# Up projection of a hybrid decoder layer: a fourth home for split weights, and the convolution's taps one step sooner

## The chip, the cores and the metric

The kernel runs as one program on one core of a Trainium2 chip. The metric is the device time of one execution in microseconds (us). The core's engines work side by side, each through a queue of its own: TensorE (PE, matrix products, with its weight loads, PEld), VectorE (DVE), ScalarE (ACT), GpSimd (POOL), and SyncE (SP), which here issues nearly all transfers (DMA) from the chip's memory. Engines wait for each other by semaphores.

## The reference

One layer, batch 1, 256 tokens, width 2048, everything in float32. The part that matters here is the second half, a gated MLP with a causal convolution over three tokens:

```python
h = rmsnorm(x, norm_ffn_w[l])
gate, up = jnp.split(jnp.einsum('bsd,df->bsf', h, w_up[l]), 2, axis=-1)
gate = causal_dwconv(gate, conv_ffn_w[l]) + conv_ffn_b[l]
x = x + jnp.einsum('bsf,fd->bsd', jax.nn.gelu(gate, approximate=False) * up, w_down[l])
```

`w_up` is 2048 x 11264: 5632 columns of gate and 5632 of up. Ahead of it come the two token mixers (a gated delta rule and a causal pooling mixer) with their projections, behind it the down projection and a last norm. The change touches none of these.

## The kernel before

**Split weights.** Float32 products are made on PE from two parts. A weight tile `raw` (128 x 1024, 512 KB) is cast on ACT to a high part `whi` (L289), and DVE makes the low part `wlo` = raw − whi, the *split* (L297). PE then multiplies by the high part first and by the low part behind it (L1374). `raw` has four buffers, `whi` and `wlo` three each. A transfer into a `raw` buffer waits for the split of the tile that lay there, four tiles earlier. A cast into a `whi` buffer waits until PE has used the tile three earlier. `weights()` hands PE the next step's parts, and before that begins (loads, casts, splits) the steps up to AHEAD = 2 further on:

```python
def weights(ahead=AHEAD):
    begin(taken[0] + ahead + 1)
    taken[0] += 1
    return made[taken[0] - 1]
```

**Chunks and steps.** The up projection runs over 11 chunks c of 512 gate and 512 up columns. PE's order is written out by hand (`up_steps`); on ACT, DVE and the queues the order comes from a scheduler, which places each instruction when its operands and its buffer are expected to be ready, and from `issue_after`, which binds one instruction behind another. In chunks 1 to 7 and 9 one half of the contraction (two blocks of 512 rows, written /1 and /0) isn't multiplied plainly: seven products of sums of quarters take the place of eight. So one *group* of PE steps, which I name after the chunk whose plain steps open it, is: g1 to g4 (the four plain gate steps of chunk c, 12 matmuls each), u1 (the first plain up step), then the parts of chunk c+1, six matmuls each, between the other up steps: T1/1, u2, 11/1, u3, T1/0, 11/0, u4, T2/1, T2/0, 21/1, 21/0, the transposes of c's gate, T3/1, T3/0, 22/1, 22/0, the transposes of c's up, T4/1, T4/0. Plain steps load a `raw` tile; parts read quarters (`quad`) that were loaded ahead to homes of their own, or sums of quarters that DVE makes (L230, bound behind the last split). The same 22 steps come again for each group.

**What else is on DVE and ACT.** Behind the products "11" a bank is copied on ACT; ahead of "21" (L1396) and behind T3 (L1410) DVE adds a bank to the product T1, and the parts behind it go on adding to that new bank. When the last T4 of a group is out, a generator `elementwise` is set up. The plain steps that follow call it, one stage at a time: `gate_part` gives four blocks of columns, each with a convolution start on ACT (L1326) and two taps on DVE (L1331), and after these the gelu on ACT (L1335); `up_part` then multiplies by up (L1344) and splits the result into `hhi` (ACT, L1351) and `hlo` (DVE, L1352). Before the change the generator stops after the second block and after the gelu:

```python
            if f == 1:
                yield
```

Each result chunk c from 4 on has a home of its own, tags `hhi4` to `hhi10`, empty until chunk c is made. Tag `s` is another place of the same size.

Of the kernel before, what the change touches and what calls it, by code (L numbers as in the profile page):

```python
# [15 lines left out]
S = 256  # L16
# [19 lines left out]
def kernel(  # L36
# [91 lines left out]
    for step in up_steps:  # L128
        if step[0] == "plain":
            srcs.append(up_w[step[1]][step[2]][step[3]])  # L130
        elif step[0] == "part":
            srcs.append(("up", *step[1:]))
    sums_behind = {}
    for n, src in enumerate(srcs):
# [138 lines left out]
    def begin_half(n, k):  # L273
        high_half(n, k)
        low_half(n, k)

    def begin(n):
        while len(made) < min(len(srcs), n):
            load(len(made) + 1)
            raw = loads[len(made)]  # L280
            if isinstance(raw, tuple):
# [4 lines left out]
            keep = kept.get(len(made))  # L286
            hi = wpool.tile(shape, F32R, tag="whi", name=nm("whi")) if keep is None else \
                mtile(keep, shape, F32R, nm("khi"))
            nc.scalar.copy(hi, raw)  # L289
            if shape[1] == 8:  # L290
                lo = None
                nc.vector.tensor_tensor(hi[:, :, 32:64], raw[:, :, 0:32], hi[:, :, 0:32].bitcast(F32),
                                        op=ALU.subtract)
            else:
                lo = wpool.tile(shape, F32R, tag="wlo", name=nm("wlo")) if keep is None else \
                    mtile(4 + keep, shape, F32R, nm("klo"))
                last_split[0] = nc.vector.tensor_tensor(lo, raw, hi.bitcast(F32), op=ALU.subtract).ins  # L297
# [1021 lines left out]
    def gate_part(c, pts):  # L1319

        y = fp.tile([P, 4, S], F32, tag="y", name=nm("y"))
        for f in range(4):
            r = 4 * c + f
            pt = pts[f // 2][:, f % 2, :]
            with tc.issue_after(last_copy[0]) if c < NUP - 1 else ExitStack():
                nc.scalar.activation(y[:, f, :], pt, AF.Identity, scale=cfw[:, 2 * KF + r : 2 * KF + r + 1],  # L1326
                                     bias=vec[:, V_CB + r : V_CB + r + 1])
            with tc.issue_after(last_sum[0]) if c < NUP - 1 else ExitStack():
                for j in (1, 0):
                    s = 2 - j  # L1330
                    nc.vector.scalar_tensor_tensor(y[:, f, s:], pt[:, : S - s], cfw[:, j * KF + r : j * KF + r + 1],  # L1331
                                                   y[:, f, s:], op0=ALU.mult, op1=ALU.add)
            if f == 1:
                yield
# [42 lines left out]
    def up_product(c, what, ch):  # L1377
# [69 lines left out]
    for i, step in enumerate(up_steps):  # L1447
        if step[0] == "part":
            up_product(*step[1:])
            if step[2] == "T4" and step[3] == chunks_of[step[1]][-1]:  # L1450
# [227 lines left out]
```

## Time and profile before

| | |
|---|---|
| three runs | 1540.68, 1541.54, 1542.59 us |
| median | 1541.54 us |
| profiled execution | 1542.63 us, of which the span is 1540.8 |
| PE busy | 1526.0 us, 99% of the span |
| DVE busy | 1253.4 us, 81% |
| ACT busy | 849.8 us, 55% |
| up projection, with the first steps behind it | 820 to 1310 us of the span |

A row of a timeline gives the start in us, the length, engine, line, operation, what it writes and reads, and shapes; "x2" means that neighbouring instructions were drawn together; a bracket at the end is the idle time before it and what ended that. A matmul's row ends when its result is drained, so that neighbouring matmuls overlap. A row of waits gives an engine's line, what it waited for, the total, the number and the longest. Buffer numbers are left out of the names in profile rows.

### The profile page before, as it was taken

The numbers are of one execution on the slowest core, as the hardware profiler recorded it, in microseconds if no ns is written. First come the engines' busy times: TensorE is split into PE (matmuls) and PEld (weight loads), VectorE is DVE, ScalarE is ACT, GpSimd is POOL, SyncE is SP. The second block draws the span as 40 slices with busy tenths as digits, with TensorE's granted clock in tenths as the row PEclk, the third lists the DMA queues.
The fourth block names the chain that finished last, engine by engine and source line by source line (L and its number), as shares of the span: only waits on it lengthen the run. The fifth ranks groups of instructions, "written<-read, shape, count | busy, mean of one in ns | idle before, by whom it ended". The sixth has DMA issues, their size and how long they took to land.

```text
span 1540.8 us, 20209 instructions
## 1 busy us (share of the span) xinstructions
PE 1526.0 (99%) x7302; PEld 1257.4 (82%) x7302; DVE 1253.4 (81%) x1776; ACT 849.8 (55%) x1063; POOL 70.8 (5%) x90
## 2 busy tenths in 40 slices
PE   9999999999999999999999999999999999999998
PEld 8887888788878888788888888888788888888886
DVE  6788859896589858987667899999999886878885
ACT  7455446454455445454455676666667665555552
POOL 1010002000100000000000000000000000000100
PEclk9999999999999999999999999999999999999999
DMA  8776757776577766776578646666457467556652
GB/s 276 215 221 199 202 163 214 213 214 183 152 245 205 205 169 201 222 200 186 179 250 300 194 163 217 219 205 205 150 155 242 125 216 267 183 193 205 227 189 90
DMA packets 166674, 310.46 MB, mean 201 GB/s; under 512 B 19458, under 2 KB 23330, under 8 KB 166446
## 3 DMA queue, kind: packets, MB, share of 16 engines
q1 hardware_dynamic: 159456, 287.37, 60.0%
q0 software_dynamic: 5184, 18.88, 3.7%
q10 hardware_dynamic: 1934, 2.93, 0.5%
q8 instruction: 57, 0.93, 0.2%
q14 instruction: 43, 0.35, 0.1%
HBM read 301.75 MB, written 7.38 MB: 201 GB/s over the span
## 4 chain that ended last, share of the span: by engine, by line
PE 92%; DVE 4%; issue 2%; DMA 1%; ACT 0%; POOL 0%; POOLq 0%; DVEq 0%; ACTq 0%
PE psg L1374 25%; PE psm L334 15%; PE psm L332 14%; PE psm L333 14%; PE psm L1359 7%; PE psg L1359 7%; DVE wlo L297 3%; PE psm L1374 2%; PE psm L478 1%; PE psg L377 1%; DVE quad L230 1%; PE psm L1436 1%; DMA vrow<-ev 1%; PE psg L868 1%; DMA mv<-vrow 1%
## 5 line engine op out<-in xcount | busy, mean ns | idle before, releaser
L289 ACT CAST whi<-raw 128x1024 fp32r<-128x1024 f32 x428 | 450.0, 1052 | 428.4 <-PE psm L333 280.2
L297 DVE TENSOR_TENSOR wlo<-raw,whi 128x1024 fp32r<-128x1024 f32 x426 | 517.3, 1220 | 151.2 <-ACT whi L289 146.2
L289 ACT CAST whi<-quad 128x1024 fp32r<-128x1024 f32 x168 | 176.1, 1054 | 141.0 <-DVE quad L230 39.4
L297 DVE TENSOR_TENSOR wlo<-quad,whi 128x1024 fp32r<-128x1024 f32 x168 | 202.6, 1219 | 36.2 <-ACT whi L289 35.3
L334 PE MATMUL psm<-wlo,xhl 128*128 128x512 f32 x432 | 169.5, 393 | 1.6 <-DVE wlo L297 1.6
L332 PE MATMUL psm<-whi,xhl 128*128 128x512 f32 x432 | 169.0, 391 | 0.0
L333 PE MATMUL psm<-whi,xhl 128*128 128x512 f32 x432 | 168.6, 390 | 0.0
L1374 PE MATMUL psg<-whi,fhl 128*128 128x512 f32 x504 | 127.1, 389 | 0.0
L1374 PEld LDWEIGHTS psg<-whi,fhl 128*128 128x128 f32 x504 | 94.4, 188 | 19.5
L334 PEld LDWEIGHTS psm<-wlo,xhl 128*128 128x128 f32 x432 | 81.1, 188 | 19.0 <-DVE wlo L297 2.4
L333 PEld LDWEIGHTS psm<-whi,xhl 128*128 128x128 f32 x432 | 81.1, 188 | 16.8
L332 PEld LDWEIGHTS psm<-whi,xhl 128*128 128x128 f32 x432 | 81.1, 188 | 16.6
L230 DVE TENSOR_TENSOR quad<-quad,quad 128x1024 f32<-128x1024 f32 x72 | 87.6, 1217 | 0.0
L1374 PE MATMUL psg<-wlo,fhl 128*128 128x512 f32 x252 | 69.9, 389 | 0.0
L1374 PE MATMUL psg<-whi,ups 128*128 128x512 f32 x216 | 58.9, 394 | 0.0
L1359 PE MATMUL psm<-whi,hhi 128*128 128x512 f32 (+1 forms) x150 | 58.1, 387 | 0.0
L1359 PE MATMUL psm<-whi,hlo 128*128 128x512 f32 (+1 forms) x150 | 57.9, 386 | 0.0
L1359 PE MATMUL psm<-wlo,hhi 128*128 128x512 f32 (+1 forms) x150 | 57.4, 387 | 0.1
L1374 PEld LDWEIGHTS psg<-wlo,fhl 128*128 128x128 f32 x252 | 47.3, 188 | 9.8
L332 PE MATMUL psm<-whi,mhi 128*128 128x512 f32 x128 | 50.8, 397 | 0.0
L1359 PE MATMUL psg<-whi,hhi 128*128 128x512 f32 (+1 forms) x130 | 50.3, 387 | 0.4 <-ACT whi L289 0.4
L1359 PE MATMUL psg<-whi,hlo 128*128 128x512 f32 (+1 forms) x130 | 50.0, 386 | 0.0
(432 smaller groups left out, 2927.3 us busy)
## 6 DMA issues: line engine op xcount, KB each, us to landing
raw<-in_w_in_dram SPq DMA_DIRECT2D x224, 512.0 KB, 4.2
raw<-in_w_up_dram SPq DMA_DIRECT2D x104, 512.0 KB, 4.8
quad<-in_w_up_dram SPq DMA_DIRECT2D x72, 512.0 KB, 4.9
raw<-in_w_down_dram SPq DMA_DIRECT2D x64, 512.0 KB, 4.7
raw<-in_w_out_dram SPq DMA_DIRECT2D x32, 512.0 KB, 4.2
quad<-in_w_down_dram POOLq DMA_DIRECT2D x24, 512.0 KB, 5.5
mv<-vrow SPq DMA_DIRECT2D x12, 512.0 KB, 4.9
taps<-in_conv_qkv_w_dram SPq DMA_DIRECT2D x16, 256.0 KB, 6.8
```

The costliest lines, as they stand in the source:

```text
L230: nc.vector.tensor_tensor(out_, plus_, minus_, op=ALU.subtract)
L289: nc.scalar.copy(hi, raw)
L297: last_split[0] = nc.vector.tensor_tensor(lo, raw, hi.bitcast(F32), op=ALU.subtract).ins
L332: mm(ps[:, t, :], lh(k, t), hi[:, kk, :], start=(k == 0), stop=False)
L333: mm(ps[:, t, :], ll(k, t), hi[:, kk, :], start=False, stop=False)
L334: mm(ps[:, t, :], lh(k, t), lo[:, kk, :], start=False, stop=(k == nk - 1))
L377: nc.tensor.transpose(pt[:, ff, t * P : (t + 1) * P], src[:, t, f * P : (f + 1) * P], ident)
L478: mm(ps_k0[:, t, :], part(k, t), w[:, kk, :], start=(k == 0 and w is hi and part is xh), stop=(k == KD - 1 and w is lo))
L868: mm(pg0, kq[:, h, 0, 0:P], kq[:, h, :, :], start=True, stop=True)
L1359: mm(ps[:, cs], lhs(kk), part_[:, kk, cs], start=(first and kk == 0 and n == 0), stop=(last and kk == 1 and n == 2), skip_group_check=shared)
L1374: mm(ps, lhs(kk), w[n][:, kk], start=(first and n == 0 and kk == 0 and lhs is high), stop=False, skip_group_check=True)
L1436: nc.tensor.transpose(out_[f // 2][:, f % 2, t * P : (t + 1) * P], e[:, t, f * P : (f + 1) * P], ident)
```

## The change

Six things are changed, all in the up projection.

1. Two windows of steps (`DEEP`) have a fourth home. From two steps behind the first (1, T4) to the first (6, T3), every fourth step begun has its high part in the place of `hhi5` and its low part in `s`; from behind the last (6, T4) to the first (8, T3) the high part lies in `hhi7`. These are places whose own results aren't made yet. The other three of four steps rotate through the three buffers as before. `raw` keeps its four.
2. In the windows, `weights()` begins one step more ahead.
3. The sum of T1 is written down four PE steps ahead of its mark instead of three, for chunks 2 to 8.
4. The add ahead of "21" is written before `weights()` instead of after it.
5. For chunks below 7, `gate_part` also stops after the first and third block, and the generator is called for the first time right where it is set up, at the last T4. So taps come one PE step sooner, and `up_part` one later.
6. A cast and split that are begun are bound behind the last convolution start and tap written so far (`last_conv`).

```diff
+    DEEP = ((first_part(1, "T4") + 2, first_part(6, "T3"), "hhi5"),
+            (1 + max(n for (c_, what_, _), n in part_at.items() if (c_, what_) == (6, "T4")), first_part(8, "T3"), "hhi7"))
+
+    def deep(n):
+        return next(((n - a, tag) for a, b, tag in DEEP if a <= n < b), None)
...
-        begin(taken[0] + ahead + 1)
+        begin(taken[0] + ahead + (2 if deep(taken[0] + ahead + 1) else 1))
...
+            behind_conv = ExitStack()
+            for ins in last_conv.values():
+                behind_conv.enter_context(tc.issue_after(ins))
+            fourth = deep(len(made))
+            if fourth and fourth[0] % 4 == 3:
+                hi = fp.tile(shape, F32R, tag=fourth[1], name=nm("whi"))
+            else:
+                fourth = None
+                hi = wpool.tile(shape, F32R, tag="whi", name=nm("whi")) if keep is None else \
+                    mtile(keep, shape, F32R, nm("khi"))
             nc.scalar.copy(hi, raw)
...
+                if fourth:
+                    lo = fp.tile(shape, F32R, tag="s", name=nm("wlo"))
...
                 last_split[0] = nc.vector.tensor_tensor(lo, raw, hi.bitcast(F32), op=ALU.subtract).ins
                 splits.append(last_split[0])
+            behind_conv.close()
...
-            if f == 1:
+            if c < 7:
+                last_conv.update(act=act_, tap=tap)
+            if f == 1 or c < 7 and f in (0, 2):
                 yield
...
+        if begins and what == "21":
+            bank[1, 0] = pg()
+            last_sum[0] = nc.vector.tensor_tensor(bank[1, 0], bank[0, 1], bank["own"], op=ALU.add).ins
         w = weights()
...
-        elif what == "21":
-            bank[1, 0] = pg()
-            last_sum[0] = nc.vector.tensor_tensor(bank[1, 0], bank[0, 1], bank["own"], op=ALU.add).ins
...
                 work[:] = [elementwise()]
+                if step[1] in range(1, 8):
+                    next(work[0], None)
...
-                if n - 3 == i:
+                if n - (4 if 2 <= step[1] <= 8 else 3) == i:
                     up_sum(step[1], "T1", chunks_of[step[1]][0])
```

On PE, SP and POOL the instructions stand in the same order before and after. On ACT and DVE their number is the same, and only the order in the up projection differs. New line numbers: the split L297 is L321, the sum of quarters L230 is L241, the cast L289 is L310, the taps L1331 are L1356, the multiplication L1344 is L1372, the split of hlo L1352 is L1380, the adds L1396 and L1410 are L1417 and L1438.

**DVE at the end of a group.** The first row is the split of T3/0 in the group of chunk 4, then come the splits of 22/1, 22/0, T4/1, T4/0, and of the next group's g1 (the one that reads `raw`). Before:

```order
L297 TENSOR_TENSOR wlo_8757<-quad_8487,whi_8755 128x1024
L230 TENSOR_TENSOR quad_8413<-quad_8452,quad_8413 128x1024
L297 TENSOR_TENSOR wlo_8779<-quad_8440,whi_8777 128x1024
L230 TENSOR_TENSOR quad_8485<-quad_8528,quad_8485 128x1024
L297 TENSOR_TENSOR wlo_8792<-quad_8501,whi_8790 128x1024
L1410 TENSOR_TENSOR psg_8800<-psg_8652,own_8688 128x512
L1331 SCALAR_TENSOR_TENSOR y_8883<-psm_8766,cfw,y_8883 128x255
L297 TENSOR_TENSOR wlo_8806<-quad_8413,whi_8804 128x1024
L297 TENSOR_TENSOR wlo_8818<-quad_8485,whi_8816 128x1024
L1331 SCALAR_TENSOR_TENSOR y_8883<-psm_8766,cfw,y_8883 128x254
L297 TENSOR_TENSOR wlo_8839<-raw_8835,whi_8837 128x1024
```

After, at the same place:

```order
L321 TENSOR_TENSOR wlo_8751<-quad_8493,whi_8749 128x1024
L241 TENSOR_TENSOR quad_8418<-quad_8456,quad_8418 128x1024
L321 TENSOR_TENSOR wlo_8762<-quad_8444,whi_8760 128x1024
L241 TENSOR_TENSOR quad_8491<-quad_8534,quad_8491 128x1024
L321 TENSOR_TENSOR wlo_8784<-quad_8511,whi_8782 128x1024
L321 TENSOR_TENSOR wlo_8796<-quad_8418,whi_8794 128x1024
L1438 TENSOR_TENSOR psg_8804<-psg_8657,own_8692 128x512
L1356 SCALAR_TENSOR_TENSOR y_8869<-psm_8771,cfw,y_8869 128x255
L321 TENSOR_TENSOR wlo_8810<-quad_8491,whi_8808 128x1024
L321 TENSOR_TENSOR wlo_8824<-raw_8820,whi_8822 128x1024
```

The split of T4/1 has moved ahead of the add, and one tap less stands ahead of g1's split.

**DVE around u1.** The first row is the split of g4 (before) in the group of chunk 4; wlo_8559 is u1, wlo_8582 is T1/1, wlo_8603 is u2, wlo_8619 is 11/1. Before:

```order
L297 TENSOR_TENSOR wlo_8534<-raw_8530,whi_8532 128x1024
L1331 SCALAR_TENSOR_TENSOR y_8521<-psm_8404,cfw,y_8521 128x255
L1331 SCALAR_TENSOR_TENSOR y_8521<-psm_8404,cfw,y_8521 128x254
L297 TENSOR_TENSOR wlo_8559<-raw_8555,whi_8557 128x1024
L230 TENSOR_TENSOR quad_8413<-quad_8413,quad_8426 128x1024
L1331 SCALAR_TENSOR_TENSOR y_8521<-psm_8404,cfw,y_8521 128x255
L1331 SCALAR_TENSOR_TENSOR y_8521<-psm_8404,cfw,y_8521 128x254
L297 TENSOR_TENSOR wlo_8582<-quad_8413,whi_8580 128x1024
L1344 TENSOR_TENSOR y_8521<-psm_8464,y_8521 128x512 x2
L297 TENSOR_TENSOR wlo_8603<-raw_8599,whi_8601 128x1024
L1352 TENSOR_TENSOR hlo_8576<-y_8521,hhi_8575 128x1024
L297 TENSOR_TENSOR wlo_8619<-quad_8426,whi_8617 128x1024
```

After, from u1's split (wlo_8540) on; wlo_8560 is T1/1, wlo_8582 is u2, wlo_8607 is 11/1:

```order
L321 TENSOR_TENSOR wlo_8540<-raw_8536,whi_8538 128x1024
L241 TENSOR_TENSOR quad_8418<-quad_8418,quad_8430 128x1024
L1356 SCALAR_TENSOR_TENSOR y_8507<-psm_8409,cfw,y_8507 128x255
L1356 SCALAR_TENSOR_TENSOR y_8507<-psm_8409,cfw,y_8507 128x254
L321 TENSOR_TENSOR wlo_8560<-quad_8418,whi_8558 128x1024
L1356 SCALAR_TENSOR_TENSOR y_8507<-psm_8409,cfw,y_8507 128x255
L1356 SCALAR_TENSOR_TENSOR y_8507<-psm_8409,cfw,y_8507 128x254
L321 TENSOR_TENSOR wlo_8582<-raw_8578,whi_8580 128x1024
L1372 TENSOR_TENSOR y_8507<-psm_8470,y_8507 128x512 x2
L321 TENSOR_TENSOR wlo_8607<-quad_8430,whi_8605 128x1024
L241 TENSOR_TENSOR quad_8491<-quad_8491,quad_8493 128x1024
L1380 TENSOR_TENSOR hlo_8602<-y_8507,hhi_8601 128x1024
```

Behind u1's split there are two pairs of taps instead of one, and the split of hlo comes one part later; ahead of u1's split, between g1 and u1, there are three taps instead of four.

**DVE between the groups of chunks 6 and 7.** The first row is the split of T4/0; before, wlo_9563, wlo_9579, wlo_9593, wlo_9620 and wlo_9645 are g1, g2, g3, g4 and u1:

```order
L297 TENSOR_TENSOR wlo_9542<-quad_9209,whi_9540 128x1024
L1331 SCALAR_TENSOR_TENSOR y_9607<-psm_9490,cfw,y_9607 128x254
L297 TENSOR_TENSOR wlo_9563<-raw_9559,whi_9561 128x1024
L297 TENSOR_TENSOR wlo_9579<-raw_9575,whi_9577 128x1024
L1331 SCALAR_TENSOR_TENSOR y_9607<-psm_9490,cfw,y_9607 128x255
L297 TENSOR_TENSOR wlo_9593<-raw_9589,whi_9591 128x1024
L1331 SCALAR_TENSOR_TENSOR y_9607<-psm_9490,cfw,y_9607 128x254
L297 TENSOR_TENSOR wlo_9620<-raw_9616,whi_9618 128x1024
L1331 SCALAR_TENSOR_TENSOR y_9607<-psm_9490,cfw,y_9607 128x255
L1331 SCALAR_TENSOR_TENSOR y_9607<-psm_9490,cfw,y_9607 128x254
L297 TENSOR_TENSOR wlo_9645<-raw_9641,whi_9643 128x1024
```

After, with g4 as wlo_9603, and g1, g2, g3 and u1 as wlo_9548, wlo_9569, wlo_9585 and wlo_9626:

```order
L321 TENSOR_TENSOR wlo_9542<-quad_9215,whi_9540 128x1024
L1356 SCALAR_TENSOR_TENSOR y_9593<-psm_9490,cfw,y_9593 128x254
L321 TENSOR_TENSOR wlo_9603<-raw_9599,whi_9601 128x1024
L321 TENSOR_TENSOR wlo_9548<-raw_9544,whi_9546 128x1024
L321 TENSOR_TENSOR wlo_9569<-raw_9565,whi_9567 128x1024
L1356 SCALAR_TENSOR_TENSOR y_9593<-psm_9490,cfw,y_9593 128x255
L321 TENSOR_TENSOR wlo_9585<-raw_9581,whi_9583 128x1024
L1356 SCALAR_TENSOR_TENSOR y_9593<-psm_9490,cfw,y_9593 128x254
L321 TENSOR_TENSOR wlo_9626<-raw_9622,whi_9624 128x1024
```

g4 has moved ahead of g1. The same stands where the first window opens, between the groups of chunks 1 and 2: there too the split of g4 comes ahead of that of g1.

More of the change, by code (lines that the diff above doesn't have):

```diff
@@ L132, with first_part @@
             srcs.append(("up", *step[1:]))
+    part_at = {tuple(src[1:]): n for n, src in enumerate(srcs) if isinstance(src, tuple)}
+    def first_part(c, what="T1"):
+        return min(n for (c_, what_, _), n in part_at.items() if c_ == c and (what_ == what or what is None))
+    DEEP = ((first_part(1, "T4") + 2, first_part(6, "T3"), "hhi5"),
+            (1 + max(n for (c_, what_, _), n in part_at.items() if (c_, what_) == (6, "T4")), first_part(8, "T3"), "hhi7"))
+    def deep(n):
+        return next(((n - a, tag) for a, b, tag in DEEP if a <= n < b), None)
     sums_behind = {}
@@ L275, in begin_half @@
         low_half(n, k)
+    last_conv = {}
     def begin(n):
@@ L1325, in gate_part @@
             with tc.issue_after(last_copy[0]) if c < NUP - 1 else ExitStack():
-                nc.scalar.activation(y[:, f, :], pt, AF.Identity, scale=cfw[:, 2 * KF + r : 2 * KF + r + 1],
-                                     bias=vec[:, V_CB + r : V_CB + r + 1])
+                act_ = nc.scalar.activation(y[:, f, :], pt, AF.Identity, scale=cfw[:, 2 * KF + r : 2 * KF + r + 1],
+                                            bias=vec[:, V_CB + r : V_CB + r + 1]).ins
             with tc.issue_after(last_sum[0]) if c < NUP - 1 else ExitStack():
@@ L1330, in gate_part @@
                     s = 2 - j
-                    nc.vector.scalar_tensor_tensor(y[:, f, s:], pt[:, : S - s], cfw[:, j * KF + r : j * KF + r + 1],
-                                                   y[:, f, s:], op0=ALU.mult, op1=ALU.add)
-            if f == 1:
+                    tap = nc.vector.scalar_tensor_tensor(y[:, f, s:], pt[:, : S - s],
+                                                         cfw[:, j * KF + r : j * KF + r + 1],
+                                                         y[:, f, s:], op0=ALU.mult, op1=ALU.add).ins
+            if c < 7:
+                last_conv.update(act=act_, tap=tap)
+            if f == 1 or c < 7 and f in (0, 2):
                 yield
```

7 lines of the change are left out of this document (3 added, 4 removed).

## The prediction

> **What bounds the kernel now.** I read the page first, then the table of five stretches, then the waits of TensorE (PE) in the up projection, then the rows around one wait.
>
> ```profile
> span 1540.8 us, 20209 instructions
> PE 1526.0 (99%) x7302; PEld 1257.4 (82%) x7302; DVE 1253.4 (81%) x1776; ACT 849.8 (55%) x1063; POOL 70.8 (5%) x90
> ```
>
> PE is the bound: 1540.8 − 1526.0 = 14.8 us of its span are idle, and no PE instruction is added or taken away. So the change can win only PE's idle time in the stage that it touches. The whole up projection (820 to 1310 us) has one kind of wait on PE (idle us in total, times, longest):
>
> ```profile
> PE psg L1374 <- DVE wlo L297: 4.0, 7, 0.6
> ```
>
> Each of the seven looks like this one, in the rows of PE and of the vector engine (DVE):
>
> ```profile
> 1009.23 1.07 PE L1374 MATMUL psg<-whi,ups 128*128 128x512 f32 x4
> 1010.95 0.73 PE L1374 MATMUL psg<-wlo,ups 128*128 128x512 f32 x2 [0.64 <-DVE wlo L297]
> ...
> 1012.30 1.17 PE L1374 MATMUL psg<-whi,fhl1b 128*128 128x512 f32 x4
> ```
>
> ```profile
> 1009.67 1.22 DVE L297 TENSOR_TENSOR wlo<-quad,whi 128x1024 fp32r<-128x1024 f32 x1
> 1010.81 0.69 DVE L1410 TENSOR_TENSOR psg<-psg,own 128x512 f32<-128x512 f32 x1
> 1011.41 0.47 DVE L1331 SCALAR_TENSOR_TENSOR y<-psm,cfw,y 128x255 f32<-128x255 f32 x1
> 1011.80 2.35 DVE L297 TENSOR_TENSOR wlo<-quad,whi 128x1024 fp32r<-128x1024 f32 x2
> ```
>
> Part 22/0's four high matmuls start at 1009.23, its low ones at 1010.95, after the split (1009.67 + 1.22 = 1010.89). One matmul takes 389 ns by the page:
>
> ```profile
> L1374 PE MATMUL psg<-whi,fhl 128*128 128x512 f32 x504 | 127.1, 389 | 0.0
> ```
>
> Four in 1.07 us so keep a pace of (1.07 − 0.39)/3 = 0.227, and the low ones could have begun at 1009.23 + 4×0.227 = 1010.14. The wait costs 0.8 us, not 0.64: the row's bracket leaves out that the pipeline drains. By that measure seven cost 4.0 + 7×0.16 = 5.1 us, 0.33% of the time. This is all that there is to win.
>
> DVE is late there because of a round that closes on itself. One group (a chunk of 512 columns) per row, cut at the ends of the splits of the group's first plain gate step (g1); the columns are length, then busy (count) of PE, weight loads, DVE, ScalarE (ACT) and POOL, the clock, the DMA share and GB/s:
>
> ```profile
> 928.66:972.16 43.50, 42.89 (x198) 35.29 (x197) 41.18 (x45) 29.36 (x35) 0.00 (x0) 1.00 0.57 194
> 972.16:1015.67 43.51, 42.87 (x198) 35.27 (x197) 41.19 (x44) 29.35 (x35) 0.00 (x0) 1.00 0.58 194
> 1015.67:1059.19 43.52, 42.94 (x198) 35.36 (x197) 41.29 (x45) 29.47 (x35) 0.00 (x0) 1.00 0.57 193
> 1059.19:1103.37 44.18, 43.23 (x198) 35.24 (x197) 41.17 (x45) 29.34 (x35) 0.00 (x0) 1.00 0.56 191
> 1103.37:1146.86 43.49, 42.89 (x198) 35.30 (x197) 41.25 (x45) 29.47 (x35) 0.00 (x0) 1.00 0.48 146
> ```
>
> The clock is 1.00 and a group takes 43.5 (the fourth, with two stalls, 44.2); without the stall PE needs 43.5 − 0.8 = 42.7. DVE is busy for 41.2 of it: 2.3 us of air. Nearly all of that lies at one place, behind the first up step (u1):
>
> ```profile
> 970.94 2.35 DVE L297 TENSOR_TENSOR wlo<-raw,whi 128x1024 fp32r<-128x1024 f32 x2
> ...
> 978.78 1.22 DVE L297 TENSOR_TENSOR wlo<-raw,whi 128x1024 fp32r<-128x1024 f32 x1 [1.53 <-ACT whi L289]
> ```
>
> ```profile
> 972.19 4.55 SPq L209 DMA_DIRECT2D raw<-in_w_up_dram  x4
> ```
>
> ```profile
> 934.19 1.05 ACT L289 CAST whi<-raw 128x1024 fp32r<-128x1024 f32 x1 [1.88 <-DMA raw<-in_w_up_dram]
> 977.70 1.05 ACT L289 CAST whi<-raw 128x1024 fp32r<-128x1024 f32 x1 [1.89 <-DMA raw<-in_w_up_dram]
> 1020.51 1.05 ACT L289 CAST whi<-raw 128x1024 fp32r<-128x1024 f32 x1 [1.18 <-DMA raw<-in_w_up_dram]
> 1065.43 1.05 ACT L289 CAST whi<-raw 128x1024 fp32r<-128x1024 f32 x1 [2.58 <-DMA raw<-in_w_up_dram]
> 1108.27 1.05 ACT L289 CAST whi<-raw 128x1024 fp32r<-128x1024 f32 x1 [1.24 <-DMA raw<-in_w_up_dram]
> ```
>
> There are four raw buffers. g1's split ends at 972.16 and frees the buffer of u1; the transfer is issued at 972.19; the cast starts at 977.70, when the data are there; the split at 978.78. From the five bounds of the stretches to these five casts it is 5.53, 5.54, 4.84, 6.24 and 4.90, together 27.05. From u1's split DVE then runs almost without a gap through the parts to the next g1, and each part's cast, split and matmuls hang on it. The round is g1's split, transfer, cast, the dense stretch, g1's split; PE has room for 42.7 and the round takes 43.5, so DVE falls behind to the point where one of its splits holds PE each time.
>
> **The change part by part.** *The fourth part home* gives casts and splits one more place in the windows; in them each step is begun one step sooner. It adds no instruction, only moves some. What it doesn't add is a raw buffer: u1 still waits for g1's split. So at the place of the five casts above it wins nothing. It can win only where a cast waits for PE to leave a part home, and where DVE then waits for the cast. In the rounds those are two, in the groups of chunks 5 and 7:
>
> ```profile
> 1044.64 1.23 DVE L297 TENSOR_TENSOR wlo<-quad,whi 128x1024 fp32r<-128x1024 f32 x1 [0.61 <-ACT whi L289]
> ```
>
> ```profile
> 1132.31 1.23 DVE L297 TENSOR_TENSOR wlo<-quad,whi 128x1024 fp32r<-128x1024 f32 x1 [0.57 <-ACT whi L289]
> ```
>
> Both go: −0.61 and −0.57. Ahead of the first window's round, in the group of chunk 2, DVE waits for casts more often:
>
> ```profile
> DVE wlo L297 <- ACT whi L289: 3.0, 6, 0.9
> ```
>
> That is from 890 to 916 us. [...]
>
> *The price of being early.* The last plain gate step (g4) can take the fourth home before g1 gets its own, and stands ahead of g1 on DVE twice: where the first window opens, and between the groups of chunks 6 and 7. The pace from one split to the next is 2.35 − 1.22 = 1.13, so g1's split, and with it u1's transfer, comes 1.13 later.
>
> ```profile
> 882.54 1.22 DVE L297 TENSOR_TENSOR wlo<-raw,whi 128x1024 fp32r<-128x1024 f32 x1
> ...
> 890.48 1.22 DVE L297 TENSOR_TENSOR wlo<-raw,whi 128x1024 fp32r<-128x1024 f32 x1 [0.58 <-ACT whi L289]
> ```
>
> At the first: g1 would end at 882.54 + 1.22 + 1.13 = 884.89, u1's cast 27.05/5 = 5.41 later at 890.30, its split 1.08 after (978.78 − 977.70) at 891.38: +0.9 against 890.48.
>
> *Taps one PE step sooner.* A pair of taps lasts 0.99, of which 0.9 is its pace (one ends as the next has begun):
>
> ```profile
> 981.06 0.99 DVE L1331 SCALAR_TENSOR_TENSOR y<-psm,cfw,y 128x255 f32<-128x255 f32 x2
> ```
>
> In the order, the stretch from one group's last "21" split to the next g1 has one tap less, the stretch from g1 to u1 one tap less, and the stretch behind u1 a pair more. One tap off the path to g1 saves its pace, 1011.80 − 1011.41 = 0.39. The tap between g1 and u1 stood in the shadow of the transfer: it cost nothing there, and behind u1, where DVE is dense, it costs. So the pair there is 0.9 on the path, less a wait that goes because the low part of the result (hlo) is now asked for a part later:
>
> ```profile
> 986.33 1.23 DVE L1352 TENSOR_TENSOR hlo<-y,hhi 128x1024 fp32r<-128x1024 f32 x1 [0.43 <-ACT hhi L1351]
> ```
>
> Per round −0.39 + 0.90 − 0.43 = +0.08. In the first group two pairs come in, with no tap gone from ahead of them: +1.8.
>
> *The second add behind T4/1's split.* The split now starts at 1010.81 in place of 1011.80, and the add begins one pace (1.13) later at 1011.94 and ends at 1012.63; part T4/1 on PE, which adds into that bank, began at 1012.30. Where DVE is as late as here, that is a wait of up to +0.33, once: a later one is inside the same round. The split of 22/0, which holds PE now, stands where it stood.
>
> *The rest is costed at nothing.* T1's sum is made one step earlier in program order, but on DVE it stands at the same place, behind u1's split. The add ahead of "21" likewise. SP's and POOL's queues keep their order, so no load is moved past another; their issue times follow the splits. The binding behind the last tap and activation changes the order only as counted. ACT's gate evictions come behind the gelu and a cast, some two casts (2×1.05) later; what covers this is the time until their bank is written again, u1, T1/1 and u2, and by 0.227 a plain step of 12 matmuls is 2.7 and a part of 6 is 1.4, so 6.8 us are there; without that cover it would be 2.1 a group.
>
> **The sum**, at the end of the last stalled group. Opening of the first window: +0.9 (g4 first) +1.8 (two pairs) −2.4 (the waits of 3.0 but for the 0.58 ahead of u1, which is in the +0.9) = +0.3. Four rounds of +0.08: +0.3. Wait in chunk 5's group: −0.6. Between chunks 6 and 7, g4 first +1.13, the pair less hlo's wait +0.47 with no tap gone ahead of g1, and the wait of 0.57 gone: +1.0. Add: +0.3. Together **+1.3 us**. The profiled execution took 1542.63 (span 1540.8 and 1.8 around it), 1.1 above the median of 1541.54; it becomes 1543.9, and against the median I predict **1542.8 us**. The unknown sizes: the two openings, between no loss (the gaps swallow g4: −2.0) and none of the 2.4 gained (+2.4); the add between 0 and 0.33 in each of six groups (5 more, +1.7); the transfers. For these five, a third row of the page has the middle time from issue to landing of all of them:
>
> ```profile
> raw<-in_w_up_dram SPq DMA_DIRECT2D x104, 512.0 KB, 4.8
> ```
>
> At 4.84 each, the shortest, the five take 24.2, which is 2.85 less: 1539.9. At 6.24, the longest, 31.2, or 4.15 more: 1546.9. I take the ones measured, since SP's queue keeps its order.
>
> **The rivals.** *Faster by up to all stalls.* The 2.4 us of waits in chunk 2's group turn into a lead that DVE keeps, g4 goes unnoticed (−2.0 in all), and the transfers come a little sooner because the casts ahead do: 1538 by the sum (1542.8 − 2.0 − 2.85). If u1's round fell by the stall's 0.8, that is from a mean of 5.41 to 4.6, PE would never wait: 1541.54 − 5.1 = 1536.4. For: DVE has 2.3 us of air a group and needs 0.8. Against: four buffers of raw data, and no transfer of the five under 4.84. [...] *Slower.* u1's transfer, asked for later and beside other quarters in flight, takes the 6.24 of chunk 6 in every group: 1546.9. It decides as soon as the five take over 28.8 together, 1.8 more than now (+1.3 and +1.8 make 3.1). For: one of five does so already; against: SP's order is the same. *Nothing happens*: the waits that the fourth home removes are not on the round, and the taps even out: 1541.5, inside my range.
>
> **How the numbers follow.** A gain or loss under 0.2% (3.1 us: 1538.5 to 1544.6) can't be told from none by measuring this kernel. My sum (0.40) and the rival of no effect (0.12) lie inside: 0.52. Faster 0.20: 0.15 for the lead with earlier transfers, 0.05 for all stalls gone. Slower 0.28: 0.20 for the transfers, 0.08 for openings and adds at their dear ends. The range, 1537.6 to 1547.0, leaves out 0.1 at each end; within the likeliest case it is 1539.9 to 1544.6.
>
> **What would show it.** Right: PE's waits for splits stay 4 to 6 us between 820 and 1310; u1's cast still waits for its transfer in each group, 4.8 to 6.2 after g1's split; the waits of DVE at 1044.64 and 1132.31 are gone; groups stay at 43.3 to 43.8; the add ends after T4/1 could start. Wrong: groups of 42.7 with no stall (faster rival), or u1's casts over 5.8 after g1's split on average, or a wait of PE on banks that ACT empties late (slower).

## The result, and the profile after

The changed kernel takes 1538.45 us (median of 22 runs, 1536.12 to 1540.66) against 1541.20 for the kernel before (22 runs). The ratio is 0.998, with a 95% interval of 0.9974 to 0.9986: 2.75 us faster, 0.18%. The prediction was 1542.8 us, 1.3 us slower, with a range from 1537.6 to 1547.0. The time lies in the range, on the other side of no change.

The first rows of the page after, and the waits of PE from 820 to 1310 us (us in total, times, longest):

```profile
span 1537.5 us, 20193 instructions
PE 1526.4 (99%) x7302; PEld 1258.7 (82%) x7302; DVE 1252.5 (81%) x1776; ACT 846.7 (55%) x1063; POOL 70.8 (5%) x90
```

```profile
PE psg L1402 <- DVE wlo L321: 0.5, 2, 0.2
PE psm L1402 <- DVE y L1356: 0.3, 1, 0.3
```

PE is as busy as before to 0.4 us. What went are its waits: 4.0 us in seven places are now 0.8 us in three. From the start of the first to the start of the last matmul of the up projection (the line L1374 before, L1402 after) PE takes 475.83 us in place of 479.26; that is −3.4, and the rest of the program gives 0.1 back.

A word on names: in all the texts here, the prediction's too, a group carries the number of the chunk whose parts stand in it, and not, as was said ahead of the prediction, of the chunk whose plain steps open it. In the kernel's own count the plain steps of "the group of chunk 3" belong to chunk 2, and its parts to chunk 3.

The groups of chunks 3 to 7, cut as before at the ends of g1's splits (at 1100.76 g4's split goes ahead of g1's, so this bound is a split later, and of the last two rows only the mean counts):

```profile
927.60:970.43 42.83, 42.58 (x196) 34.84 (x195) 41.16 (x44) 29.14 (x34) 0.00 (x0) 1.00 0.61 204
970.43:1013.07 42.64, 42.64 (x198) 35.47 (x197) 41.35 (x45) 29.25 (x35) 0.00 (x0) 1.00 0.57 191
1013.07:1056.19 43.12, 42.90 (x198) 35.31 (x197) 41.27 (x44) 29.35 (x35) 0.00 (x0) 1.00 0.60 201
1056.19:1100.76 44.57, 44.57 (x206) 37.09 (x205) 42.69 (x46) 30.57 (x36) 0.00 (x0) 1.00 0.57 191
1100.76:1142.73 41.97, 41.96 (x194) 34.62 (x193) 39.55 (x42) 27.96 (x33) 0.00 (x0) 1.00 0.46 145
```

They add up to 215.13 us against 218.20 before. DVE is busy for 206.03, against 206.08. DVE does the same work in a shorter time, so its amount of work isn't what held the groups at 43.5.

**Where the lead is lost.** A *home* is the pair of buffers that the high and the low part of one step lie in. The *high lead* at a step is the time from the end of its cast to PE's first high matmul, the *low lead* the time from the end of its split to PE's first low matmul. What changed can be seen at part 21/0, from which DVE's work is dense up to 22/0, where PE stood still. Before, in the group of chunk 4, in rows of ACT, PE and DVE:

```profile
998.11 1.06 ACT L289 CAST whi<-quad 128x1024 fp32r<-128x1024 f32 x1 [0.66 <-PE psg L1374]
999.07 1.07 ACT L1427 COPY e<-psg 128x512 f32<-128x512 f32 x2
1000.02 1.07 ACT L289 CAST whi<-quad 128x1024 fp32r<-128x1024 f32 x1
```

```profile
998.82 1.07 PE L1374 MATMUL psg<-whi,ups 128*128 128x512 f32 x4
...
1002.90 1.07 PE L1374 MATMUL psg<-whi,fhl 128*128 128x512 f32 x4
1003.81 0.62 PE L1374 MATMUL psg<-wlo,fhl 128*128 128x512 f32 x2
```

The cast of 21/0 ends at 1001.09, behind one that had waited 0.66 us for PE to leave a home and behind two copies. Its own home is that of T2/1, three steps earlier, whose high matmuls are the first PE row: they end at 998.82 + 1.07 = 999.89, so the copies held the cast (1000.02) up by at most 0.13. PE's first high matmul of 21/0 starts at 1002.90: a high lead of 1.81 us. The split leads the low matmuls by 1003.81 − 1002.35 = 1.46:

```profile
1001.12 1.23 DVE L297 TENSOR_TENSOR wlo<-quad,whi 128x1024 fp32r<-128x1024 f32 x1
```

After, at the same part:

```profile
997.81 1.06 ACT L310 CAST whi<-quad 128x1024 fp32r<-128x1024 f32 x1 [0.61 <-PE psg L1402]
```

```profile
995.80 1.98 PE L1402 MATMUL psg<-whi,fhl 128*128 128x512 f32 x8
...
1002.60 1.07 PE L1402 MATMUL psg<-whi,fhl 128*128 128x512 f32 x4
1003.50 0.63 PE L1402 MATMUL psg<-wlo,fhl 128*128 128x512 f32 x2
```

```profile
998.90 1.23 DVE L321 TENSOR_TENSOR wlo<-quad,whi 128x1024 fp32r<-128x1024 f32 x1
...
1007.46 2.35 DVE L321 TENSOR_TENSOR wlo<-quad,whi 128x1024 fp32r<-128x1024 f32 x2
```

The cast ends at 998.87: a high lead of 3.73, which is 1.92 more. With four homes 21/0 takes that of u4, four steps earlier, whose high matmuls (the first PE row) end at 995.80 + 1.98 = 997.78. This is 4.82 ahead of 21/0's own, where T2/1's ended 3.01 ahead: 1.81 of the 1.92. The rest is that the copies now stand behind the cast. The split ends at 1000.13, a low lead of 3.37. From there to the end of 22/0's split DVE needs as long as before: 1007.46 + 1.21 = 1008.67, which is 8.54 later (before, 1002.35 to 1010.89: 8.54). PE takes 6.33 from 21/0's low matmuls to 22/0's where it doesn't wait (1003.81 to 1010.14). So a low lead of 2.2 us at 21/0 is wanted. Three homes gave 1.46, and PE waited the difference, 0.75; four give up to 3.4 (2.1 to 3.4 in the six groups).

That the lead is a cap, and not what a round happens to leave, shows in all six groups (read from the casts and first high matmuls of 21/0, us; the transfer is from the split that frees its buffer, g1's or in the last after g4's, to u1's cast):

| | high lead at 21/0, groups of chunks 2 to 7 | u1's transfer, groups of chunks 3 to 7 |
|---|---|---|
| before | 1.82, 1.82, 1.81, 1.82, 1.82, 1.82 | 5.53, 5.54, 4.84, 6.24, 4.90 |
| after | 3.73 in all six | 4.89, 4.01, 4.90, 4.96, 5.16 |

Before, the transfer differed by 1.4 us and the high lead by 0.01. Only behind the longest transfer (6.24, group of chunk 6) was DVE later than the cap allows: its low lead was 0.79 there, and PE had a second stall, of 0.34 us.

### The profile page after: what moved, and what is told of

The parts are those of the page before. It is cut to its first block, busy times and chain, and to the rows that moved or that the text cites. A ratio compares the mean times of both kernels' runs of the same rounds, so it can differ in the third digit from the quotient of the medians.

```text
span 1537.5 us, 20193 instructions
## 1 busy us (share of the span) xinstructions
PE 1526.4 (99%) x7302; PEld 1258.7 (82%) x7302; DVE 1252.5 (81%) x1776; ACT 846.7 (55%) x1063; POOL 70.8 (5%) x90
## 5 line engine op out<-in xcount | busy, mean ns | idle before, releaser
L310 ACT CAST whi<-raw 128x1024 fp32r<-128x1024 f32 x428 | 449.6, 1052 | 428.1 <-PE psm L358 280.7
L321 DVE TENSOR_TENSOR wlo<-raw,whi 128x1024 fp32r<-128x1024 f32 x426 | 516.8, 1220 | 154.2 <-ACT whi L310 149.1
L310 ACT CAST whi<-quad 128x1024 fp32r<-128x1024 f32 x168 | 175.7, 1053 | 138.0 <-PE psg L1402 44.8
L321 DVE TENSOR_TENSOR wlo<-quad,whi 128x1024 fp32r<-128x1024 f32 x168 | 203.1, 1219 | 32.6 <-ACT whi L310 31.3
L1402 PE MATMUL psg<-whi,fhl 128*128 128x512 f32 x504 | 127.2, 390 | 0.0
L1402 PEld LDWEIGHTS psg<-whi,fhl 128*128 128x128 f32 x504 | 94.5, 188 | 19.6
L241 DVE TENSOR_TENSOR quad<-quad,quad 128x1024 f32<-128x1024 f32 x72 | 87.6, 1217 | 0.0
L1402 PE MATMUL psg<-wlo,fhl 128*128 128x512 f32 x252 | 69.9, 390 | 0.0
L1402 PE MATMUL psg<-whi,ups 128*128 128x512 f32 x216 | 58.8, 394 | 0.0
L1402 PEld LDWEIGHTS psg<-wlo,fhl 128*128 128x128 f32 x252 | 47.3, 188 | 9.9
```

The lines of the kernel that those rows point to most:

```text
L241: nc.vector.tensor_tensor(out_, plus_, minus_, op=ALU.subtract)
L1402: mm(ps, lhs(kk), w[n][:, kk], start=(first and n == 0 and kk == 0 and lhs is high), stop=False, skip_group_check=True)
```

## The experiments

Two theories. *Cap*: at 21/0 DVE can be no further ahead of PE than the homes of the parts allow; three homes allow too little. *Round* (the prediction's): a group lasts as long as g1's split, u1's transfer and DVE's dense stretch. All times below are medians, and ratios, with 95% intervals, are to the kernel before in the same runs. Line numbers move with an edit: PE's products of the up projection are L1374 before, L1402 after, and L1384, L1400 or L1412 in other kernels. The chunks that `own_raw` names are those of the plain steps, so chunks 2 to 5 are the groups named 3 to 6.

**home_only: the fourth home and the step more ahead, alone** (the change with parts 3 to 6 undone):

```diff
-            if c < 7:
-                last_conv.update(act=act_, tap=tap)
-            if f == 1 or c < 7 and f in (0, 2):
+            if f == 1:
...
-        if begins and what == "21":
...
+        elif what == "21":
...
-                if step[1] in range(1, 8):
-                    next(work[0], None)
...
-                if n - (4 if 2 <= step[1] <= 8 else 3) == i:
+                if n - 3 == i:
```

> The kernel before with the fourth home and the one step more ahead in the windows (parts 1 and 2 of the change), and nothing else of it: taps, adds, T1's sum and the binding stand as before. Cap theory: with three homes DVE's lead over PE at the split of 21/0 can never be more than 1.5 us (in the trace before it is 1.47 in five of six groups, whatever u1's transfer took), and the dense stretch behind it needs 0.6 to 0.8 more; a fourth home lifts the cap by about a part (1.36 us), so the stalls at 22/0 go without the rest of the change: 3 to 4.5 us faster than before, groups of 42.7 us. Round theory (the prediction's): the pace is g1's split, u1's transfer, the dense stretch; the fourth home does not shorten it: within 1 us of before, stalls at 22/0 still there, groups of 43.5.

1539.00 us, ratio 0.9983 (0.9975 to 0.9992). The stalls at 22/0 are gone but for 0.06 us at one place; 2.0 us of other waits stand in five places, three of them on the add behind T3. The gain is 2.2 us, less than the 3 to 4.5 of the cap theory. But here T1's cast is written ahead of T1's sum, so T1 is made of a quarter and not of the difference of two; nothing waits for that sum, and this time says little without the next run.

**home_sum: the same with T1's sum one step earlier** (parts 1, 2 and 3; against home_only):

```diff
-                if n - 3 == i:
+                if n - (4 if 2 <= step[1] <= 8 else 3) == i:
```

> Parts 1, 2 and 3 of the change alone: the fourth home, the step more ahead, and T1's sum one step earlier, which the step more ahead needs; taps, adds and binding as before. Cap theory: the lead in front of 21/0's high matmuls is 3.73 us as in the change and not 1.82, the stalls at 22/0 go; what the taps and the add had to do (three waits of 0.23 us on the add behind T3 and one of 0.6 us on a tap, seen where the fourth home stood alone without T1's earlier sum) stays: 2 to 3 us faster than before, 0.3 to 1 us short of the change. Round theory: as before within 1 us.

1563.81 us, ratio 1.0144 (1.0130 to 1.0158). Both theories fail: 22.6 us slower. The high lead is 3.73 in each group and 22/0 waits in one group only (0.8 us, behind the end of the first window), as the cap theory has it, but T1/1 waits 17.4 us in five places for a tap. The run home_alone, further down, takes this up.

**no_fourth: everything but the home and the step ahead** (parts 3 to 6):

```diff
-            if fourth and fourth[0] % 4 == 3:
+            if fourth and fourth[0] < 0:
...
-        begin(taken[0] + ahead + (2 if deep(taken[0] + ahead + 1) else 1))
+        begin(taken[0] + ahead + 1)
```

> The changed kernel without its fourth home and without the one step more ahead (parts 3 to 6 alone). Cap theory: the lead at 21/0 is 1.5 us again and the stalls at 22/0 are back, about 0.8 us in each of six groups: 0 to 1.5 us slower than before, so 3 to 4 us slower than the change. Round theory, in the form that the trace after would ask for (u1's transfer begins one tap sooner and waits less): the gain stays without the fourth home, 2 to 3 us faster than before.

1541.62 us, ratio 1.0000 (0.9991 to 1.0008). PE's waits in the up projection:

```profile
PE psg L1402 <- DVE wlo L321: 3.6, 6, 0.6
```

The high lead is 1.82 in each of the six groups again and each has its stall. u1's transfers took 5.24, 4.95, 5.10, 5.05 and 4.66, together 25.0, 2 us less than before: no gain came of it. The gain needs these two parts; home_not_ahead, further down, says which.

**early_u1: u1's transfer out of the round, three homes** (on the kernel before; `own_raw` holds the steps u1 of chunks 2 to 5):

```diff
...
+            if n in own_raw:
+                loads.append(fp.tile(list(srcs[n].shape), F32, tag="hlo5", name=nm("raw")))
+            else:
...
```

> The kernel before, but u1's raw tile of the chunks 2 to 5 lies in an empty home of its own (that of hlo5), so that its transfer waits for no split of g1 and is done long before; the order on PE, ACT and DVE is that of before. Round theory: the round of these four groups falls from 43.5 to under 42.7, so PE's stalls in them go: 3 to 3.5 us faster. Cap theory: u1's split comes sooner, but the next casts wait for PE to leave a home, the lead at 21/0 is 1.5 us as before and the stalls at 22/0 stay at 0.6 (bracket): within 0.5 us of before.

1541.36 us, ratio 0.9997 (0.9988 to 1.0007). The order on PE, ACT and DVE is unchanged, and u1's cast now waits for a home instead of for data:

```profile
1019.02 1.05 ACT L299 CAST whi<-raw 128x1024 fp32r<-128x1024 f32 x1 [0.57 <-PE psg L1384]
```

```profile
PE psg L1384 <- DVE wlo L307: 3.6, 6, 0.6
```

The high lead at 21/0 is 1.82 in each group, and the stalls are those of before except for the second one in chunk 6's group, which is gone. From one g1's split to the next the four groups take 43.5 us each. The round theory falls here: by it they would have become 0.8 us shorter each.

**late_u1: u1's transfer later, four homes** (on the changed kernel; `own_raw` holds g2 and u1 of chunks 2 to 5, which so share one place):

```diff
...
+            if n in own_raw:
+                loads.append(fp.tile(list(srcs[n].shape), F32, tag="hlo5", name=nm("raw")))
+            else:
...
```

> The changed kernel, but in the chunks 2 to 5 u1's raw tile lies in the place where g2's lay (the home of hlo5), so that its transfer waits for g2's split and comes behind those of u2 and u3 in the queue, some 2 to 4 us later. Round theory: each of the four rounds gets longer by that, 6 to 12 us in all less the slack of the groups (0.8 each): 5 us or more slower than the change. Cap theory: the lead at u1 is 5 to 7 us and is cut down to the cap at 21/0 anyway: within 1 us of the change, so still 2 us or more faster than before.

1546.97 us, ratio 1.0032 (1.0020 to 1.0045), 8.5 us slower than the change. u1's cast waits 4.5 to 5.0 us for its data in three groups, and the low lead at 21/0 falls to 0.8, 1.4 and 0.6 there. The cap theory's forecast, within 1 us of the change, fails here, and the round theory's comes true. So with four homes the transfer does count: the lead is the lesser of what the homes allow and what the round leaves, and with three homes the cap was the lesser one (but for the longest transfer). This run doesn't give a clean price, since the order on ACT and DVE changed with it in several groups, and one group lost 2.9 us at another part, behind which PE ran at half pace for 3.1 us (see the last section).

**home_alone: the home alone, nothing further ahead** (part 1 on the kernel before; against home_only):

```diff
-        begin(taken[0] + ahead + (2 if deep(taken[0] + ahead + 1) else 1))
+        begin(taken[0] + ahead + 1)
```

> Part 1 of the change alone on the kernel before: the fourth home, nothing begun further ahead, taps, T1's sum, adds and binding as before. If the home is all that counts: lead in front of 21/0 3.7 us, no stall at 22/0, 2.5 to 4 us faster than before. If the taps sooner and the binding (parts 5 and 6) are what makes a deeper lead safe, as the run with parts 1, 2 and 3 suggests (waits of T1/1's matmuls on the last tap of 1.9 to 4.3 us in five groups, 22 us in all): casts and splits slip ahead of convolution starts and taps on ACT and DVE, T1/1 waits for the taps to leave their bank, and the time is at best that of before, at worst 20 us more.

1563.33 us, ratio 1.0140 (1.0123 to 1.0156). PE's waits from 820 to 1310 us, and DVE and PE at T1/1 in the group of chunk 3:

```profile
PE psm L1400 <- DVE y L1356: 17.9, 5, 4.3
PE psg L1400 <- DVE wlo L321: 0.8, 1, 0.8
```

```profile
937.34 1.22 DVE L321 TENSOR_TENSOR wlo<-raw,whi 128x1024 fp32r<-128x1024 f32 x1
938.47 0.48 DVE L1356 SCALAR_TENSOR_TENSOR y<-psm,cfw,y 128x254 f32<-128x254 f32 x1
938.86 1.22 DVE L321 TENSOR_TENSOR wlo<-quad,whi 128x1024 fp32r<-128x1024 f32 x1
940.00 1.22 DVE L241 TENSOR_TENSOR quad<-quad,quad 128x1024 f32<-128x1024 f32 x1
941.13 0.48 DVE L1356 SCALAR_TENSOR_TENSOR y<-psm,cfw,y 128x255 f32<-128x255 f32 x1
941.53 1.21 DVE L321 TENSOR_TENSOR wlo<-raw,whi 128x1024 fp32r<-128x1024 f32 x1
942.66 1.22 DVE L241 TENSOR_TENSOR quad<-quad,quad 128x1024 f32<-128x1024 f32 x1
943.79 0.47 DVE L1356 SCALAR_TENSOR_TENSOR y<-psm,cfw,y 128x254 f32<-128x254 f32 x1
```

```profile
939.22 1.07 PE L1400 MATMUL psg<-wlo,fhl2a 128*128 128x512 f32 x4
944.41 1.62 PE L1400 MATMUL psm<-whi,ups 128*128 128x512 f32 x3 [4.12 <-DVE y L1356]
```

With a home free, the scheduler lets casts and splits go ahead of convolution starts and taps. The taps read the gate's transposes from one of the two banks of `psm`; T1/1 wants that bank, and the last tap leaves it at 944.26. PE stands still for 4.1 us, though the parts it will want are ready.

**home_not_ahead: the home, the taps sooner and the binding, without the step more ahead** (the change without part 2):

```diff
-        begin(taken[0] + ahead + (2 if deep(taken[0] + ahead + 1) else 1))
+        begin(taken[0] + ahead + 1)
```

> The changed kernel with its fourth home, but weights() begins no more steps ahead than before. If the home alone lifts the cap (a cast waits for nothing but its home), the lead at 21/0 and the time are those of the change within 0.7 us. If the step more ahead is what does it (the scheduler places a cast only where the program has asked for it), the lead at 21/0 stays near 1.5 us, the stalls at 22/0 are back, and the time is that of before within 1 us.

1537.51 us, ratio 0.9977 (0.9968 to 0.9986). The high lead is 3.69 to 3.73. So it is the home that lifts the cap, and the step more ahead adds nothing: PE's stretch from first to last matmul is 474.83 us, against 475.83 in the change.

**no_bind: the change without the binding** (part 6):

```diff
-            if c < 7:
-                last_conv.update(act=act_, tap=tap)
```

> The changed kernel without part 6: casts and splits are no longer bound behind the last convolution start and tap; taps one step sooner as in the change. If the binding is what keeps splits from slipping ahead of the taps: waits of T1/1 on a tap of 1 to 4 us in several groups, slower than before by 5 us or more. If the taps written one step sooner are enough by themselves: the time of the change within 1 us.

1563.42 us, ratio 1.0143 (1.0126 to 1.0159), with 17.1 us of waits for taps in five places.

**no_sooner: the change without the taps sooner** (part 5; the binding stays):

```diff
-            if f == 1 or c < 7 and f in (0, 2):
+            if f == 1:
...
-                if step[1] in range(1, 8):
-                    next(work[0], None)
```

> The changed kernel without part 5's taps one step sooner; the binding of part 6 stays, behind taps that are now written a step later. If the earlier taps are what is needed: waits of T1/1 on a tap come back, slower than before by 5 us or more. If the binding is enough: the time of the change within 1 us.

1539.90 us, ratio 0.9989 (0.9980 to 0.9998). No wait for a tap; 2.0 us of waits for splits in five places. So the binding is what keeps the home from doing harm. That the earlier taps add anything is not shown: the medians differ by 1.5 us, the intervals overlap, and PE's stretch is 477.12, against 475.83 and 476.85 in two executions of the change.

**after_again: the change once more.**

> The changed kernel once more, on the same chip as the three others and with its own trace: 2 to 3.5 us faster than before, as measured. Its trace says how far u1's transfer differs from one execution to the next: if the five took 4.0 to 5.0 us by the kernel's doing, they do so again; if by chance, they lie elsewhere between 3.9 and 6.2.

1538.37 us, ratio 0.9979 (0.9970 to 0.9988). u1's transfers took 5.68, 4.64, 5.21, 4.53 and 5.53 (the last again from g4's split), together 25.6, where the first execution had 23.9 and the kernel before 27.1: they vary by execution. Where it took 5.68 the low lead at 21/0 fell to 1.84, under the 2.2 that is wanted, and one of that group's parts behind it has a stall of 0.68 us again:

```profile
962.78 0.73 PE L1402 MATMUL psg<-wlo,ups 128*128 128x512 f32 x2 [0.68 <-DVE wlo L321]
```

**after_early7: u1's transfer out of the round, four homes** (the changed kernel; `own_raw` holds u1 of chunks 2 to 7):

```diff
...
+            if n in own_raw:
+                loads.append(fp.tile(list(srcs[n].shape), F32, tag="hlo5" if n < DEEP[0][1] else "hlo7", name=nm("raw")))
+            else:
...
```

> The changed kernel with u1's raw tile of the chunks 2 to 7 in an empty home of its own (those of hlo5 and hlo7), so that its transfer waits for no split; the order on PE, ACT and DVE is that of the change. Cap theory with the round behind it: in the change the low lead at 21/0 is 2.1 to 3.4 us, mostly under the cap of 3.4, so with four homes u1's transfer does count; with it out of the way the lead is 3.4 in each group and the last stalls (0.25 us twice at T4/0, one at 22/0) go: 0.5 to 1.5 us faster than the change, 3.3 to 4.5 faster than before. Cap theory alone (the transfer never matters): within 0.4 us of the change. Without the fourth home the same edit moved nothing.

1537.20 us, ratio 0.9974 (0.9964 to 0.9983); the low lead is 3.1 to 3.4 in the five groups of chunks 3 to 7. The time is 1.2 us under that of the change, but the intervals overlap; the trace has 0.6 us of waits on PE left.

**mix and mix_turn.** mix is after_early7 without the step more ahead (the edit of home_not_ahead). mix_turn is mix with T4/0's split bound behind T4/1's; against mix:

```diff
-                last_split[0] = nc.vector.tensor_tensor(lo, raw, hi.bitcast(F32), op=ALU.subtract).ins
+                in_turn = isinstance(src, tuple) and src[0] == "up" and src[2:] == ("T4", 0) and src[1] in TWO
+                with tc.issue_after(last_split[0]) if in_turn else ExitStack():
+                    last_split[0] = nc.vector.tensor_tensor(lo, raw, hi.bitcast(F32), op=ALU.subtract).ins
```

> The changed kernel without part 2 (no step more ahead) and with u1's raw tile in an empty home (chunks 2 to 7), the two edits that were each about 1 us better than the change in the runs before. If both gains are real and come from the same few remaining stalls (0.25 us twice at T4/0, one at 22/0, one at T1/1): 1536.5 to 1537.5, no better than either alone. If they are of separate causes: 1536 or under.

> The run called mix, with one split bound: that of T4/0 behind that of T4/1 (in two groups the scheduler has them the other way round, and PE waits 0.25 us there for T4/1's split). If that order is the cause of the last two stalls, PE waits for no split in the rounds any more: 0.3 to 0.6 us faster than mix, which is near what can be told apart; the trace tells it better than the time.

mix: 1537.45 us, 0.9972 (0.9959 to 0.9984), with the two waits of 0.25 us at T4 left. mix_turn: 1536.61 us, 0.9966 (0.9953 to 0.9979), and PE waits nowhere from 820 to 1310 us; its stretch is 473.54 us. It is the fastest of all: 4.7 us under the kernel before. Its interval and that of the change overlap a little, so that it beats the change is shown by the trace (no wait left) and not by the time alone.

## Why the prediction was wrong

- *All that there is to win is 5.1 us of stalls.* Right, nearly. With no stall left, mix_turn gained 4.7 in the median; in its profiled execution PE's stretch is 5.7 us shorter than before.
- *A round through u1's transfer sets the pace.* Wrong, and this is the step that failed. It was read from one place where DVE waits (978.78) and from the length of a round that came out as 43.5. "Nearly all" of DVE's 2.3 us of air was said to lie there; the row has 1.53. The rows quoted there spoke against it: u1's cast came 5.54 and 4.84 after g1's split in two groups that both took 43.5. A round that sets the pace would have passed the 0.7 on. Taking the transfer out (early_u1) moved nothing. And in the change itself u1's cast still waits for its transfer, by 2.1 to 4.2 us in each of the five groups, while the stalls are gone: the sign that was named for a right forecast couldn't tell. In its place the runs show this: the high lead at 21/0, held at 1.82 us by casts that wait for a home, is short of what DVE's stretch behind it takes.
- *The fourth home wins nothing at that place and only two waits of 0.6 in the rounds.* Wrong for the same reason. Those two waits, at 1044.64 and 1132.31, are the splits of 21/0: they were the cap itself, seen where the transfer had been quick enough for DVE to run into it. They were costed as waits of DVE to be saved, where they were the mark of what holds DVE back. The rival with a lead that DVE keeps came nearest; it had 0.15. Its 1538 us is partly luck, though: 2.85 us of its gain were to come from sooner transfers, which early_u1 and no_fourth show to be worth nothing with three homes. The gap at 22/0 stood in all six groups (waits of 0.58 to 0.64 us) and went with one more home: the only waits for splits left in the trace after from 820 to 1310 us, 0.25 and 0.22, are at T4/1.
- *The sum.* From the first matmul of the up projection to the first behind the last stalled group PE takes 322.76 us, against 326.95 before: −4.2 where +1.3 was forecast. Of this, −0.6 falls to the opening in chunk 2's group, where the forecast was +0.3. Behind the last stalled group 0.8 is lost again, 0.35 of it a wait of chunk 8's T1 for a tap; what makes up the rest isn't shown.
- *The transfers as measured, since SP's queue keeps its order.* The order was kept, the times weren't: the five took 27.1, 23.9 and 25.6 us in three executions. With three homes none of that decided the time (early_u1, no_fourth).
- *g4 ahead of g1 delays u1's transfer by 1.13, twice (+0.9 and +1.13).* Wrong. The buffer goes to u1 when the first of the group's splits frees one, whichever that is: in the trace after g4's split runs from 883.47 to 884.68 and u1's transfer is issued at 884.71, before g1's split ends at 885.82.

```profile
884.71 1.50 SPq L220 DMA_DIRECT2D raw<-in_w_up_dram  x2
```

- *A tap off the stretch to g1 (−0.39), a pair in behind u1 less hlo's wait (+0.47).* The sizes were right: 13.33 became 12.94 from 21/0's split to g1's in four of six groups, and the stretch from u1's split to 21/0's got 0.36 longer in the first of the rounds. But both lie where DVE has a lead, so they set the lead and not the time.
- *The second add behind T4/1's split costs +0.33 once.* Right in kind: in two executions of the change T4/1 began 0.24 and 0.43 us later than in the other groups, once each, behind this add.
- *The binding changes the order only as counted, at no cost.* The price was right, but what the binding is for was missed: without it (no_bind) splits overtake the taps that hold T1's bank, and the kernel is 25 us slower than the change.
- *A change under 0.2% can't be told from none.* Wrong for 22 runs of each: the 0.18% here stand clear of no change, with an interval of 0.14 to 0.26%.

## What to carry to other kernels

Where an engine is late at the same step in every round, look not only for the wait ahead of it that is longest, but measure its lead over the consumer at a fixed step in all rounds. A lead that stays the same in every round (here to 0.01 us) while the transfers ahead of it differ (here by 1.4 us) points to a cap by buffers. Then the buffers' count, not the transfer, is what to change; a run that takes the transfer away, and one that takes only the buffer away, show which it is. And a freer producer can take the place of other work in its queue, as splits took that of the taps in home_alone, where PE then waited 17.9 us for taps: before giving it a buffer, look which bank or buffer that other work holds, and bind the producer behind it.

## What was unexpected of the hardware

Waits of PE cost more than their length here once they were long. In four kernels here (home_alone, home_sum, no_bind and late_u1) a pause of 3.3 to 4.9 us between the starts of two matmuls (13 of them) was followed by matmuls at a pace of 427 ns in place of 227, until 3.1 to 5.7 us after the pause; behind four pauses of 2.1 to 2.2 us the pace stayed. Around the wait of 4.1 us shown for the home alone, the granted clock (the column behind POOL) was 1.00 ahead of the wait, 0.50 in the 4.5 us behind it and 0.98 after that:

```profile
930.00:939.00 9.00, 9.00 (x42) 7.44 (x41) 5.95 (x8) 5.33 (x7) 0.00 (x0) 1.00 1.04 389
944.50:949.00 4.50, 4.50 (x11) 3.53 (x12) 2.72 (x4) 2.91 (x3) 0.00 (x0) 0.50 0.26 99
949.00:958.00 9.00, 9.00 (x41) 7.39 (x40) 6.40 (x6) 5.00 (x6) 0.00 (x0) 0.98 0.21 60
```

That is why 17 to 18 us of waits made a kernel 22 us slower although its other stalls, 4 us, were gone. An estimate for the home alone: behind its four long pauses PE ran at about half pace for 17.3 us in all and so lost 8.7; these, its waits of 17.9 and 0.8, less the 5.1 that the stalls cost before, make 22.3. PE's stretch grew by 22.3, from 479.26 to 501.58. The shortest pause with the slow pace behind it was 3.28 us between starts, 2.89 us of it idle (late_u1); the clock granted there from 1056.80 to 1060.00 was 0.51. What a pause between 2.2 and 3.28 us does, no run shows.
